# Conditioning columns of a feed-forward layer: where in the layer each of them is reduced

## The chip, the cores and the metric

The kernel runs on one core of a Trainium2 chip. Its time is the device time of one execution in microseconds; several executions of the same program are timed and their median is taken. One further execution is recorded by the hardware profiler, and all rows below come from that one.

## The reference

Three network blocks run one after another on 256 tokens of width 1024: a two-layer block, a block with a recurrence and 32 experts, and a third block. The part that matters here is the feed-forward of the two layers of the first block, and one product of the second block that does not depend on the tokens:

```python
def swiglu(x, w_gate, w_up, w_down):          # 1024 -> 2816 -> 1024, in layer 0 and layer 1
    return (jax.nn.silu(x @ w_gate) * (x @ w_up)) @ w_down

x = layer_norm(ALPHA * x + swiglu(x, w_gate, w_up, w_down), g, b)
...
cond = jax.nn.silu(c)                          # second block: one row of 1024
mod = cond @ ada_w + ada_b                     # 6 * 1024 outputs; the third block has 3 * 1024 more
```

The first 2048 outputs of `mod` are made elsewhere. The other 7168 are 56 columns of 128, each a sum over 1024 products per output.

## The kernel before

**Products in two parts.** Every large weight comes by DMA as float32 and is split into a high part `wh` (ScalarE, L338) and a low part `wl` (L342: every third unit of the feed-forward on GpSimd, the others on VectorE). A unit is 128x1024 numbers of a weight. TensorE then makes three products for each pair (`xh wh`, `xl wh`, `xh wl`), all recorded under L555. The splits are recorded up to three units ahead of the unit that TensorE is at, and four buffers of each of `wh` and `wl` go round.

**The feed-forward, `ffn_ple`.** Its 2816 inner columns are done in six groups `q`: five of 512 columns and a last of 256. In each group the gate product (`dense_F`) is followed by the SiLU on ScalarE (L1153), and the up product by a multiplication on VectorE that reads the up result out of PSUM (`sg<-sg,acc`, L1161) and by a split into `hh` (ScalarE, L593) and `hl` (VectorE, L594). A group of 512 has four units for the gate and four for the up product, the last group two and two. Then `residual` puts ALPHA times the old activations into four PSUM tiles (`acc<-alphaI,xf`, 32 matmuls), and the down product adds 22 units to them (`rows_T`, one unit for each step `k`). PSUM tiles of the name `acc` go round in four buffers: the first three tiles of `residual` take buffers that have long been read, and its last takes the one that the last group's up product was in, so it has to wait for L1161 of that group.

**The conditioning columns.** Each of the 56 columns is one VectorE instruction, L1274: it multiplies a tile `adat` (128x1024, weights) with the row `pe` (the SiLU of c) and sums along the row into one column of `mod2` or `mod3`. TensorE has no part in it. `adat` has three buffers: when column `m` has been recorded, `cond_load` (L1291) puts the load for column `m+3` on SyncE's DMA queue, and that queue also issues the weight loads (L325), in the order in which they were recorded; a load whose buffer isn't free holds up all behind it.

**Where the columns stand.** A table, `MODS`, says for each of the two layers how many columns are pushed at each of its places: entries 0 to 11 behind the gate and the up product of groups 0 to 5 in turn, entry 12 at step 4 of the down product, 13 at step 8, 14 at step 12, 15 at step 16 (entries 16 and 17 are never read). What is pushed at a place is recorded in the background of the next product, one column at each `tick` (one after every unit of gate and up, two in every step of the down product):

```python
            self.cond(MODS[i][2 * q], crow)                      # behind the gate product of group q
            pu = self.dense_F(f"w_ffn_up{i}", x, n=n)
            ...
            self.cond(MODS[i][2 * q + 1], crow)                  # behind the up product and its split
        ps = self.residual(xf)
        ...
        def ready(k):                                            # called at each step of the down product
            if k and k % 4 == 0 and k < NQ - 2:
                self.cond(MODS[i][11 + k // 4], crow)
```

Layer 0 makes 24 of the columns and layer 1 the other 32. The engines run what was recorded for them in that order.

Of the kernel before, what the change touches and what calls it, by code (L numbers as in the profile page):

```python
# [146 lines left out]


EXPERTS = [(1, 0)] + [x for e in range(31) for x in ((1, e + 1), (2, e))] + [(2, 31)]
MODS = [[0, 3] + [2] * 9 + [3] + [0] * 6, [0, 3] + [2] * 9 + [3] + [3, 3, 2, 0, 0, 0]]  # L150


def weight_plan(stages):
# [271 lines left out]
class KB:  # L425
# [709 lines left out]
    def ffn_ple(self, i, xf, x, ready):  # L1135
# [3 lines left out]
        if "mod" in self.stages:  # L1139
            self.push("cond", self.cond_sum(P, i))  # L1140
            crow = self.cond_rows(P, i)
            self.apool = P
            self.ada_end += sum(MODS[i])
        pt = self.tl(P, [128, 2, T], F32, "pt")
# [3 lines left out]
        for q in range(6):  # L1148
# [5 lines left out]
            for _ in range(3 if q == 0 else 0):  # L1154
                self.cond_load()
            self.cond(MODS[i][2 * q], crow)
            pu = self.dense_F(f"w_ffn_up{i}", x, n=n)
            for j in range(n // 256):
# [3 lines left out]
                self.split(gj, hh[:, s], hl[:, s])  # L1162
            self.cond(MODS[i][2 * q + 1], crow)
        ps = self.residual(xf)
# [26 lines left out]
        def ready(k):  # L1191
            if k and k % 4 == 0 and k < NQ - 2:
                self.cond(MODS[i][11 + k // 4], crow)

# [1437 lines left out]
```

## Time and profile before

| | us |
|---|---|
| median of 3 runs | 2259.61 |
| the runs | 2253.85 to 2260.05 |
| the profiled execution | 2253.87 |
| its span, first to last instruction | 2252.1 |
| TensorE busy in the span | 2122.8 (94%) |
| VectorE busy | 1073.3 (48%) |
| ScalarE busy | 724.5 (32%) |
| GpSimd busy | 269.1 (12%) |

Times in the rows are counted from the start of the span. The feed-forward of layer 0 lies between about 227 and 422 us, that of layer 1 between about 564 and 758 us; the experts' weights stream from 1100 to 2000 us. A timeline row gives the start, the busy time, the engine, the line, what was written from what, and in brackets the idle time of the engine just before, with the instruction that ended it.

### The profile page before, as it was taken

What the parts mean: (1) busy time and instruction counts of PE and PEld (TensorE: products, weight loads), DVE (VectorE), ACT (ScalarE), POOL (GpSimd) and SP (SyncE); (2) the same over time, 40 slices, a digit from 0 to 9 for tenths busy, and PEclk for the clock granted to TensorE, in tenths of its full rate; (3) what the DMA queues carried; (4) which work ended last, traced back from release to release, by engine and by line L of the source; (5) the groups of instructions that cost most, each with busy time, mean ns of one, the idle gap of its engine ahead of it and who ended that gap; (6) DMA issues with size and microseconds to landing.
All of it is one profiled execution on the core that took longest, in us unless ns stands there. A gap on an engine that the chain in (4) does not pass through costs nothing. (4 is left out here: it accounts for less than half of the span.)

```text
span 2252.1 us, 31704 instructions
## 1 busy us (share of the span) xinstructions
PE 2122.8 (94%) x13258; PEld 1489.4 (66%) x13258; DVE 1073.3 (48%) x2013; ACT 724.5 (32%) x1169; POOL 269.1 (12%) x144
## 2 busy tenths in 40 slices
PE   8999999999999988799899999999999999999996
PEld 8997997887997878688444444334433333368886
DVE  6775775566787567746222222322221111245665
ACT  5444543554543454343111110111111111133552
POOL 2322232100232012310000000000000000004101
PEclk9999999999999999999899999999999999999999
DMA  7334785332787433105799999999999999984320
GB/s 295 150 146 158 309 315 206 152 150 86 312 319 271 176 122 113 38 1 219 324 426 427 427 423 427 427 428 427 427 428 427 428 427 427 427 333 161 119 76 20
DMA packets 65652, 618.06 MB, mean 274 GB/s; under 512 B 8128, under 2 KB 10176, under 8 KB 19808
## 3 DMA queue, kind: packets, MB, share of 16 engines
q1 hardware_dynamic: 62320, 612.33, 66.5%
q10 hardware_dynamic: 3184, 3.65, 0.5%
q8 instruction: 106, 1.74, 0.3%
q14 instruction: 42, 0.34, 0.0%
HBM read 614.90 MB, written 1.05 MB: 274 GB/s over the span
## 5 line engine op out<-in xcount | busy, mean ns | idle before, releaser
L555 PE MATMUL acc<-xh,wh 128*128 128x256 f32 (+1 forms) x1736 | 487.5, 285 | 7.3 <-ACT wh L338 2.8
L555 PE MATMUL acc<-xl,wh 128*128 128x256 f32 (+1 forms) x1736 | 482.2, 281 | 2.9 <-DVE xl L594 1.5
L555 PE MATMUL acc<-xh,wl 128*128 128x256 f32 (+2 forms) x1704 | 476.4, 280 | 5.3 <-DVE wl L342 5.3
L555 PE MATMUL acc<-expert,xe 128*64 128x512 f32 x2000 | 447.7, 598 | 17.7 <-DMA expert<-exp_w 17.7
L342 DVE TENSOR_TENSOR wl<-w,wh 128x1024 fp32r<-128x1024 f32 x202 | 270.1, 1346 | 155.3 <-ACT wh L338 154.8
L338 ACT ACTIVATE wh<-w 128x1024 fp32r<-128x1024 f32 (+1 forms) x263 | 274.0, 1054 | 213.7 <-PE acc L555 176.0
L555 PEld LDWEIGHTS acc<-xh,wh 128*128 128x128 f32 (+1 forms) x1736 | 326.5, 189 | 16.2 <-issue 5.6
L555 PEld LDWEIGHTS acc<-expert,xe 128*64 128x64 f32 x2000 | 140.5, 137 | 294.8 <-issue 275.5
L555 PEld LDWEIGHTS acc<-xl,wh 128*128 128x128 f32 (+1 forms) x1736 | 328.8, 191 | 7.5 <-DVE xl L594 3.5
L555 PEld LDWEIGHTS acc<-xh,wl 128*128 128x128 f32 (+2 forms) x1704 | 322.5, 189 | 7.1 <-DVE wl L342 6.9
L555 PE MATMUL py<-expert,aT 128*64 128x512 f32 x1024 | 234.3, 600 | 3.6 <-DMA expert<-exp_w 2.8
L342 POOL TENSOR_TENSOR wl<-w,wh 128x1024 fp32r<-128x1024 f32 (+1 forms) x61 | 153.4, 2515 | 527.6 <-ACT wh L338 468.4
L2069 ACT ACTIVATE s<-a 128x512 f32<-128x512 f32 x32 | 20.2, 630 | 530.1 <-DVE a L2068 530.1
L2136 DVE SCALAR_TENSOR_TENSOR xf<-py,mod,xf 128x256 f32<-128x256 f32 x128 | 55.7, 479 | 279.8 <-PE py L555 279.8
L2068 DVE TENSOR_SCALAR a<-acc 128x512 f32<-128x512 f32 x32 | 22.1, 692 | 346.2 <-PE acc L555 346.2
L555 PEld LDWEIGHTS py<-expert,aT 128*64 128x64 f32 x1024 | 72.0, 138 | 137.3 <-issue 127.8
L342 POOL TENSOR_TENSOR wl<-w_w_in,wh 128x1024 fp32r<-128x1024 f32 (+1 forms) x11 | 26.8, 2435 | 1053.8 <-ACT wh L338 1042.9
L1274 DVE SCALAR_TENSOR_TENSOR adat<-adat,pe 128x1024 f32<-128x1024 f32 x56 | 97.3, 1756 | 12.3 <-DMA adat<-tiles 12.3
L2123 ACT ACTIVATE y<-py 64x512 f32<-64x512 f32 x64 | 37.9, 592 | 117.9 <-PE py L555 117.4
L555 PE MATMUL tp<-sel,xh 128*128 128x128 f32 x512 | 63.3, 284 | 7.9 <-ACT aT L2103 6.9
L555 PE MATMUL acc<-wh,hh 128*128 128x512 f32 x176 | 69.7, 396 | 0.0
L555 PE MATMUL acc<-wl,hh 128*128 128x512 f32 x176 | 69.4, 394 | 0.0
(641 smaller groups left out, 2856.2 us busy)
## 6 DMA issues: line engine op xcount, KB each, us to landing
expert<-exp_w SPq DMA_DIRECT2D x188, 2048.0 KB, 31.3
w<-tiles SPq DMA_DIRECT2D x140, 1024.0 KB, 6.9
adat<-tiles SPq DMA_DIRECT2D x56, 512.0 KB, 7.7
w_w_in<-tiles SPq DMA_DIRECT2D x18, 1024.0 KB, 5.0
w<-exp_w SPq DMA_DIRECT2D x3, 2048.0 KB, 7.6
w_w_out<-tiles SPq DMA_DIRECT2D x4, 1024.0 KB, 4.8
expert<-exp_w SPq DMA_DIRECT2D x4, 512.0 KB, 30.1
w_w_o_moba<-tiles SPq DMA_DIRECT2D x2, 1024.0 KB, 4.7
```

The source lines that it names most:

```text
L338: kb.nc.scalar.activation(hi, w, AF.Copy)
L342: (kb.nc.gpsimd if far else kb.nc.vector).tensor_sub(lo, w, hi.bitcast(F32))
L555: self.nc.tensor.matmul(out, lhsT, rhs, start=start, stop=True, skip_group_check=True)
L1274: self.nc.vector.scalar_tensor_tensor(w, w, 1.0, crow[:, int(m >= 48)], op0=OP.mult, op1=OP.mult, accum_out=dst)
L2068: nc.vector.tensor_scalar(a, pg, 7.0, None, op0=OP.min)
L2069: nc.scalar.activation(s, a, AF.Sigmoid, scale=1.702)
L2123: nc.scalar.activation(y[r, o], py[r], AF.Copy)
L2136: nc.vector.scalar_tensor_tensor(xf[:, k], ps[o][:, c], gate2(k), xf[:, k], op0=OP.mult, op1=OP.add)
```

## The change

One table is different; no instruction is added or taken away.

```diff
-MODS = [[0, 3] + [2] * 9 + [3] + [0] * 6, [0, 3] + [2] * 9 + [3] + [3, 3, 2, 0, 0, 0]]
+MODS = [[0, 3, 2, 2, 3, 2, 2, 3, 2, 2, 0, 0] + [3] + [0] * 5, [0, 3, 2, 2, 3, 2, 2, 3, 2, 2, 0, 0] + [3, 3, 3, 2, 0, 0]]
```

In both layers the two columns behind the last gate product (group 5) and the three behind the last up product are gone from there. One more is pushed behind the gate product of group 2 and one more behind the up product of group 3. The other three go to the down product: in layer 0, which had none there, to step 4; in layer 1 the steps 4, 8, 12, 16 have 3, 3, 3, 2 instead of 3, 3, 2, 0.

First VectorE at the end of layer 0's gate and up products, before. `sg` of L1161 is the multiplication of the last group, `adat` of L1274 a column, `wl` of L342 the low part of a weight:

```order
L1274 SCALAR_TENSOR_TENSOR adat_3485,mod_15_119<-adat_3485,pe_2344 128x1024
L342 TENSOR_TENSOR wl_3711<-w_30_3297,wh_3710 128x1024
L1274 SCALAR_TENSOR_TENSOR adat_3580,mod_15_119<-adat_3580,pe_2344 128x1024
L342 TENSOR_TENSOR wl_3745<-w_30_3297,wh_3744 128x1024
L1274 SCALAR_TENSOR_TENSOR adat_3611,mod_15_119<-adat_3611,pe_2344 128x1024
L1274 SCALAR_TENSOR_TENSOR adat_3708,mod_15_119<-adat_3708,pe_2344 128x1024
L1161 TENSOR_TENSOR sg_3741<-sg_3741,acc_3743 128x512
L594 TENSOR_TENSOR hl_2349<-sg_3741,hh_2348 128x512
L342 TENSOR_TENSOR wl_3830<-w_30_3297,wh_3829 128x1024
L1274 SCALAR_TENSOR_TENSOR adat_3739,mod_15_119<-adat_3739,pe_2344 128x1024
L1274 SCALAR_TENSOR_TENSOR adat_3773,mod_15_119<-adat_3773,pe_2344 128x1024
L342 TENSOR_TENSOR wl_3851<-w_31_3426,wh_3850 128x1024
```

The same place now, VectorE:

```order
L342 TENSOR_TENSOR wl_3717<-w_30_3300,wh_3716 128x1024
L1274 SCALAR_TENSOR_TENSOR adat_3586,mod_15_119<-adat_3586,pe_2344 128x1024
L342 TENSOR_TENSOR wl_3751<-w_30_3300,wh_3750 128x1024
L1161 TENSOR_TENSOR sg_3747<-sg_3747,acc_3749 128x512
L594 TENSOR_TENSOR hl_2349<-sg_3747,hh_2348 128x512
L342 TENSOR_TENSOR wl_3830<-w_30_3300,wh_3829 128x1024
L342 TENSOR_TENSOR wl_3849<-w_31_3429,wh_3848 128x1024
L342 TENSOR_TENSOR wl_3881<-w_31_3429,wh_3880 128x1024
L342 TENSOR_TENSOR wl_3897<-w_31_3429,wh_3896 128x1024
L1274 SCALAR_TENSOR_TENSOR adat_3617,mod_15_119<-adat_3617,pe_2344 128x1024
L1274 SCALAR_TENSOR_TENSOR adat_3714,mod_15_119<-adat_3714,pe_2344 128x1024
L1274 SCALAR_TENSOR_TENSOR adat_3745,mod_15_119<-adat_3745,pe_2344 128x1024
```

Two columns no longer stand between the last split of a weight and the multiplication L1161; three stand together some units into the down product.

SyncE's queue over the same stretch, before (`w_33` is a weight tile of the down product):

```order
L325 DMA w_32_3552<-tiles 128x2048 x2
L1291 DMA adat_3580<-tiles 128x1024
L1291 DMA adat_3611<-tiles 128x1024
L325 DMA w_33_3680<-tiles 128x2048 x2
L1291 DMA adat_3708<-tiles 128x1024
L1291 DMA adat_3739<-tiles 128x1024
L1291 DMA adat_3773<-tiles 128x1024
L1291 DMA adat_3804<-tiles 128x1024
L325 DMA w_34_3833<-tiles 128x2048 x2
```

And SyncE's queue now:

```order
L1291 DMA adat_3519<-tiles 128x1024
L325 DMA w_32_3558<-tiles 128x2048 x2
L1291 DMA adat_3586<-tiles 128x1024
L1291 DMA adat_3617<-tiles 128x1024
L325 DMA w_33_3686<-tiles 128x2048 x2
L1291 DMA adat_3714<-tiles 128x1024
L1291 DMA adat_3745<-tiles 128x1024
L325 DMA w_34_3833<-tiles 128x2048 x2
```

Two column loads instead of four stand between `w_33` and `w_34`, and both belong to columns of the down product.

## Rows read from the trace of the kernel before

**Rows 1.** TensorE's waits, 225 to 480 and 560 to 770: total, times, longest

```profile
PE acc L555 <- DVE sg L1161: 5.6, 1, 5.6
...
PE acc L555 <- DVE sg L1161: 5.5, 1, 5.5
```

**Rows 2.** Timeline of TensorE, end of layer 0's up products

```profile
350.27 2.84 PE L555 MATMUL acc<-alphaI,xf 128*128 128x128 f32 x24
358.72 2.07 PE L555 MATMUL acc<-alphaI,xf 128*128 128x128 f32 x8 [5.61 <-DVE sg L1161]
360.44 0.77 PE L555 MATMUL acc<-wh,hh 128*128 128x512 f32 x1
...
364.33 0.40 PE L555 MATMUL acc<-wh,hh 128*128 128x512 f32 x1
```

**Rows 3.** Timeline of TensorE, the same place in layer 1, and its down product's end

```profile
695.82 2.08 PE L555 MATMUL acc<-alphaI,xf 128*128 128x128 f32 x8 [5.49 <-DVE sg L1161]
697.54 0.77 PE L555 MATMUL acc<-wh,hh 128*128 128x512 f32 x1
...
698.86 0.39 PE L555 MATMUL acc<-wh,hh 128*128 128x512 f32 x1
...
758.04 2.32 PE L555 MATMUL py<-pt,w 128*128 128x256 f32 x10
```

**Rows 4.** Stretches of layer 0: length, busy PE, PEld, DVE, ACT, POOL, clock, DMA, GB/s

```profile
357.50:358.00 0.50, 0.00 (x0) 0.00 (x0) 0.50 (x3) 0.00 (x0) 0.00 (x0) 0.50 0.37 148
...
364.20:366.00 1.80, 1.80 (x10) 1.47 (x9) 0.00 (x0) 0.72 (x1) 0.00 (x0) 1.00 1.03 437
```

**Rows 5.** Timeline of VectorE before the last multiplication of layer 0

```profile
348.60 1.21 DVE L342 TENSOR_TENSOR wl<-w,wh 128x1024 fp32r<-128x1024 f32 x1
349.74 3.38 DVE L1274 SCALAR_TENSOR_TENSOR adat<-adat,pe 128x1024 f32<-128x1024 f32 x1
...
356.83 1.23 DVE L1274 SCALAR_TENSOR_TENSOR adat<-adat,pe 128x1024 f32<-128x1024 f32 x1 [3.71 <-DMA adat<-tiles]
...
357.98 0.68 DVE L1161 TENSOR_TENSOR sg<-sg,acc 128x512 f32<-128x512 f32 x1
```

**Rows 6.** Timeline of VectorE, the same place in layer 1

```profile
693.93 1.23 DVE L1274 SCALAR_TENSOR_TENSOR adat<-adat,pe 128x1024 f32<-128x1024 f32 x1 [3.57 <-DMA adat<-tiles]
```

**Rows 7.** SyncE's queue, timeline; then DMA issues of 347 to 349, time to landing last

```profile
346.48 0.80 SPq L325 DMA_DIRECT2D w<-tiles  x2
347.37 11.05 SPq L1291 DMA_DIRECT2D adat<-tiles  x4
...
adat<-tiles SPq DMA_DIRECT2D x2, 512.0 KB, 9.3
```

**Rows 8.** All 56 columns: shortest, median and longest in ns

```profile
L1274 DVE SCALAR_TENSOR_TENSOR adat<-adat,pe x56: 1207/1220/3430, 257.2 to 734.5; 128x1024 f32<-128x1024 f32 x56
```

**Rows 9.** Timeline of VectorE in layer 0, groups 2 and 4: weight splits it waited for

```profile
294.39 1.22 DVE L342 TENSOR_TENSOR wl<-w,wh 128x1024 fp32r<-128x1024 f32 x1 [2.25 <-ACT wh L338]
...
330.29 1.23 DVE L342 TENSOR_TENSOR wl<-w,wh 128x1024 fp32r<-128x1024 f32 x1 [0.92 <-ACT wh L338]
...
337.86 1.22 DVE L342 TENSOR_TENSOR wl<-w,wh 128x1024 fp32r<-128x1024 f32 x1 [0.71 <-ACT wh L338]
```

**Rows 10.** Timeline of GpSimd: the last up unit's split in layer 0, and the next

```profile
343.42 3.03 POOL L342 TENSOR_TENSOR wl<-w,wh 128x1024 fp32r<-128x1024 f32 x1 [8.51 <-ACT wh L338]
348.88 3.15 POOL L342 TENSOR_TENSOR wl<-w,wh 128x1024 fp32r<-128x1024 f32 x1 [2.44 <-ACT wh L338]
```

**Rows 11.** Timeline of VectorE in layer 1's down product

```profile
721.60 3.23 DVE L1274 SCALAR_TENSOR_TENSOR adat<-adat,pe 128x1024 f32<-128x1024 f32 x1 [1.85 <-DMA adat<-tiles]
...
725.90 1.22 DVE L342 TENSOR_TENSOR wl<-w,wh 128x1024 fp32r<-128x1024 f32 x1
```

**Rows 12.** Experts' stretch, columns as in rows 4; SyncE's waits, 800 to 1110

```profile
1100.00:2000.00 900.00, 869.87 (x4197) 354.98 (x4197) 192.74 (x424) 111.61 (x209) 0.00 (x0) 0.99 1.00 423
...
SPq L412 <- PE acc L555: 31.7, 5, 19.5
```

## The prediction

> **What bounds the kernel now.** I read TensorE's waits first, since it is busy for 94% of the span. In the two stretches that hold a feed-forward, one wait stands out in each: 5.6 us and 5.5 us, both for L1161, the multiplication of an up result on VectorE [rows 1]. The other waits of those stretches are 0.5 us or less. So TensorE sets the pace there, and no weight split ever held it up.
>
> TensorE's timeline shows which multiplication it is. The first 24 of `residual`'s 32 matmuls run from 350.27 to 353.11 us; the last eight start at 358.72 [rows 2]. They need the PSUM tile of group 5's up product, which L1161 of that group frees. VectorE's timeline shows why it is late: the up product ends at 350.27, but VectorE starts a column at 349.74 that takes 3.38 us, then has another in front whose weights arrive only at 356.83, after 3.71 us of idling, and only then, at 357.98, comes L1161 [rows 5]. SyncE's queue explains the late weights: that load was issued at 347.37, behind the weight load of 346.48, and took 9.3 us to land [rows 7]. Layer 1 repeats the pattern, with 3.57 us for the load [rows 6] and 5.49 us on TensorE [rows 3].
>
> The wait costs more than itself. While TensorE sat idle its granted clock fell to half (0.50 at 357.5, which is 1.2 GHz); it is back at 1.00, 2.4 GHz, from 364.2 [rows 4], and the matmuls in between are slow.
>
> **What the change takes away.** First the waits: 5.61 + 5.49 = 11.10 us [rows 2, 3]. Then the slow matmuls.
> - At full clock, 24 of `residual`'s matmuls take 2.84 us [rows 2], so eight take 0.95; after the wait they took 360.44 - 358.72 = 1.72. Lost: 0.77 in each layer.
> - The down product at full clock: 22 units of 12 matmuls are 264, and from the fourth on 261 take 758.04 - 698.86 = 59.18 us [rows 3], 0.227 each. In layer 0 the first nine took 364.33 - 360.44 = 3.89 instead of 2.04 [rows 2]. Lost: 1.85. In layer 1 the first three took 1.32 instead of 0.68 [rows 3]. Lost: 0.64.
>
> That is 2 x 0.77 + 1.85 + 0.64 = 4.03 us, and 11.10 + 4.03 = **15.1 us** in all.
>
> **Is the wait really gone?** In the new order VectorE has, between the last multiplications of group 4 and L1161 of group 5, column, split, column, split. These are the four that now end at 349.81 [rows 5]. The up product ends at 350.27, so L1161 can start some 0.2 us later and, at 0.68 us [rows 5], is done by about 351.2. TensorE needs the tile at 353.11. The 24 matmuls that need nothing cover it with 1.9 us to spare, so I take 0 for what is left of the wait. If VectorE came to that place later than now, only what exceeds 1.9 us would be paid. Neither of the two columns still there waits for a late load: the one that did belonged to the load behind `w_33`, and in the new queue only columns of the down product are behind `w_33`.
>
> **What it costs where the columns go.** A column takes between 1.21 and 3.43 us, 1.22 in the median [rows 8]. The long ones lie beside a GpSimd split: one that begins at 349.74, with GpSimd at a split from 348.88 to 352.03, took 3.38 [rows 5, 10]. The Trainium skill (GPSIMD Engine Reference, section Specifications) says that GpSimd shares its SBUF interfaces with VectorE and that VectorE instructions with two SBUF inputs contend with it; a column has two such inputs, `adat` and `pe`. By that rule every column that meets a GpSimd split would be a long one, which speaks against putting more of them between splits. By it and the rows the five moved columns of a layer would take up to 5 x 3.43 = 17.2 us of VectorE instead of 5 x 1.22 = 6.1. The trace agrees for the long ones, but shows most columns in gaps. What follows uses both durations from the rows.
>
> - *Third column behind gate 2.* It runs during up 2. VectorE waits 2.25 us there for the next weight split [rows 9]. At 1.22 us the column fits; at 3.43 it pushes the split by 1.2 us, and splits run units ahead. I take 0.
> - *Third column behind up 3.* It runs during gate 4. VectorE's idle time from there to the end of group 4 is 0.92 + 0.71 = 1.63 us [rows 9], so 1.22 fits with little over. Behind it is the tightest place I found: group 4's multiplications release ScalarE, which then feeds GpSimd the split of the last up unit, done at 343.42 + 3.03 = 346.45 [rows 10]. That unit starts 24 matmuls before 350.27; a unit takes 12 x 0.227 = 2.72 us, so at 347.55, and first reads the low part 0.2 us later. Slack: about 1.3 us. At 1.22 the cost is 0; at 3.43 VectorE is 1.8 us late and TensorE waits 0.5 us per layer; if the column also had to wait 3.7 us for its weights, as the worst did [rows 5], it would be 5.5 - 1.3 = 4.2 us per layer. I take 0, since the two loads in question are issued well ahead in the new queue (three columns ahead, none directly behind a blocked weight load), and keep 4.2 as the end of the range.
> - *Down product.* Layer 1 already has groups of three there, with a column that waited 1.85 us for its load and then took 3.23 [rows 11], and TensorE never waited [rows 1]. How near was it? The split that followed (unit 12 of 0 to 21, counted back over VectorE's and GpSimd's splits from the last) was done at 725.90 + 1.22 = 727.12 [rows 11]; unit 12 starts ten units before 758.04 [rows 3], at 730.8. Slack 3.6 us. Layer 0's one group and layer 1's 3, 3, 3, 2 are of the same kind, and the columns that used to run at the start of the down product (the three pushed behind up 5) are gone. Cost 0; the other bound is under the rivals.
> - *Loads.* As many as before, of the same size. Column loads are earlier by one or two places in groups 2 to 4, and `w_34` no longer waits for a column of the down product's start. I take 0.
>
> **Does it reach the end?** The experts run at a DMA share of 1.00 for 900 us [rows 12], so time won before could be lost if that stream began at a fixed moment. It doesn't: before it, the expert loads wait for TensorE (31.7 us in five waits, for buffers it has to free) [rows 12], so they begin earlier by as much as TensorE does.
>
> **Sum.** The profiled execution took 2253.87 us, which is 1.77 around its span. 2253.87 - 15.1 = 2238.8. It lay 5.7 us under the median of the three runs, 2259.61; from the median, 2259.61 - 15.1 = 2244.5. I forecast **2244 us**.
>
> **Rivals.**
> - *A smaller wait replaces it.* The moved column of up 3 meets a GpSimd split and a late load, VectorE reaches group 4's multiplications late, and TensorE waits at the last up unit: 4.2 us per layer, 15.1 - 8.4 = 6.7 gained, 2252.9. For it: only 1.6 us of idle time covers the column. Against: the loads of this place are ahead by three columns. At 3.43 us without the load it would be 1.0 in all, 2245.5.
> - *Only the wait goes, the slow clock stays.* Some other break near the place, too short to count as one of the waits above, leaves the clock at half for as long as now. Gain 11.1, 2248.5. For it: the clock is the part I can't trace to one instruction. Against: the stretches before 353 and after 364 run at full clock with the same short breaks.
> - *Nothing arrives.* The gain is lost before the end, because the order of expert loads or of the third block's weights is set by something other than TensorE: 2259.6. Against: rows 12.
> - *Slower.* VectorE falls behind wherever the columns went, because each moved column is held to 3.43 us and each group waits 3.71 us for its first load. Up 3's column then costs 8.4 us in both layers. A group of three in the down product takes 3 x 3.43 + 3.71 = 14.0 us; four units of TensorE last 10.9, of which VectorE's own 8/3 splits of 1.22 take 3.3, which leaves 7.6, and the slack covers 3.6 more; 2.8 us remain for TensorE. Five such groups (counting the pair as one) are 14.0. 8.4 + 14.0 - 15.1 = 7.3 us slower, 2266.9. It outweighs the gain once columns cost about two thirds of that beyond the cover. Against: layer 1 ran such groups without a wait. The sharing that the Trainium skill states (GPSIMD Engine Reference, section Specifications) would make the longer duration the usual one wherever a GpSimd split runs.
> - *The change doesn't do what it says*, that is, something else stands in front of L1161 and is just as late. The new order shows splits alone between the last column and L1161, so I give it no chance of its own.
>
> **How the numbers follow.** Chances: forecast 0.74, smaller wait 0.10, clock 0.06, nothing 0.05, slower 0.05. The range takes in the forecast on either base (2238.8 and 2244.5) with some 3 us below, since single runs of one program here differ by up to 6 us, and reaches up to the smaller wait: 2236 to 2253. About 0.3%, 6.8 us, is what a measurement of this kernel can tell from no change. The forecast, the clock rival and the better half of the smaller wait are faster by more than that, with a little off for what I overlooked: 0.85. Within it: 0.10. Slower: 0.05.
>
> **What would show it.** In the changed profile TensorE's waits in the feed-forwards have no entry for L1161 of more than 1 us; `residual`'s 32 matmuls run as one block of some 3.8 us; the granted clock stays at 1.00 through the start of both down products; L1161 of group 5 starts right after the up product, with no column before it that waited for DMA. Wrong it would be if TensorE waits for `wl` in the last up unit, or in the down product behind a group of columns, or if the experts' stream starts at the same time as before.

## The result and the profile after

The median went from 2259.61 to **2244.0 us** (five runs, 2241.32 to 2247.12), a ratio of 0.9937 with a 95% interval of 0.9921 to 0.9953: 0.6% faster. The profiled execution took 2241.32 us.

First the waits, since the prediction hung on one of them. TensorE's waits from 225 to 480 us, then from 560 to 770 (total, times, longest):

```profile
PE py L555 <- ACT pr L1123: 1.4, 1, 1.4
PE tp L756 <- DVE xf L743: 0.5, 1, 0.5
PE acc L555 <- ACT xh L593: 0.2, 1, 0.2
...
PE acc L555 <- DVE xl L594: 0.3, 1, 0.3
```

L1161, with 5.6 and 5.5 us before [rows 1], is gone from both layers. None of what is left waits for a weight split; the 1.4 us for `pr` are not new, before has them at 486.20, outside these stretches. Then TensorE's timeline at the end of the up products of layer 0 and of layer 1, in place of [rows 2, 3]:

```profile
352.13 0.28 PE L555 MATMUL acc<-xh,wl 128*128 128x256 f32 x1
352.25 3.73 PE L555 MATMUL acc<-alphaI,xf 128*128 128x128 f32 x32
355.73 0.48 PE L555 MATMUL acc<-wh,hh 128*128 128x512 f32 x1
...
680.94 3.73 PE L555 MATMUL acc<-alphaI,xf 128*128 128x128 f32 x32
684.43 0.48 PE L555 MATMUL acc<-wh,hh 128*128 128x512 f32 x1
```

All 32 rows of `residual` are one block now, and the first matmuls of the down product start 3.48 us after it began, where before they started 10.17 us after. VectorE's timeline shows why, in place of [rows 5]: column, split, and then L1161, which waits for TensorE and no longer the other way round.

```profile
349.43 1.21 DVE L1274 SCALAR_TENSOR_TENSOR adat<-adat,pe 128x1024 f32<-128x1024 f32 x1
...
350.58 1.22 DVE L342 TENSOR_TENSOR wl<-w,wh 128x1024 fp32r<-128x1024 f32 x1
352.44 0.69 DVE L1161 TENSOR_TENSOR sg<-sg,acc 128x512 f32<-128x512 f32 x1 [0.65 <-PE acc L555]
```

To compare kernels I use one **stretch** in each layer: from the first `acc<-alphaI,xf` (the up products are done) to the first `py<-pt,w` (the down product is done). Stretches of the kernel before, with the columns of [rows 4] (length, busy PE, PEld, DVE, ACT, POOL, granted clock, DMA share, GB/s):

```profile
350.27:422.15 71.88, 66.27 (x298) 55.32 (x297) 29.84 (x38) 22.80 (x22) 16.14 (x7) 0.95 0.50 192
687.49:758.04 70.55, 65.06 (x299) 54.46 (x297) 42.94 (x54) 22.82 (x22) 16.92 (x8) 0.98 0.66 248
```

And of the kernel after:

```profile
352.25:415.67 63.42, 63.42 (x298) 53.14 (x297) 28.00 (x34) 22.80 (x22) 16.71 (x7) 1.00 0.50 202
415.67:680.94 265.27, 257.10 (x1994) 237.85 (x1992) 197.91 (x349) 145.44 (x259) 38.57 (x16) 0.99 0.55 211
680.94:744.36 63.42, 63.42 (x298) 53.14 (x297) 39.07 (x50) 22.82 (x22) 18.64 (x8) 1.00 0.67 260
```

Both layers now take the same 63.42 us, with TensorE busy for all of it at 1.00, which is 2.4 GHz: 8.46 us less in layer 0, 7.13 less in layer 1, 15.6 in all. The medians differ by 15.6 too, but that they agree to a tenth is luck: the interval of the ratio leaves 10.6 to 17.9 us. Between the two stretches nothing moved (265.27 us, and 687.49 - 422.15 = 265.34 before). The spans, 2252.1 and 2239.5, differ by only 12.6, because in code that the change doesn't touch this one execution lost 1.98 us ahead of 352.25 and 1.08 behind 744.36. Part of the first is this, at the start of layer 0's gate products, a stretch which had 1.00 before:

```profile
228.26:240.00 11.74, 11.66 (x85) 11.40 (x85) 8.28 (x14) 7.04 (x11) 0.00 (x0) 0.85 1.00 398
```

### The profile page after: what moved, and what is told of

Same layout as the page of the kernel before. It is cut to its first block, busy times and chain, and to the rows that moved or that the text cites. A ratio compares the mean times of both kernels' runs of the same rounds, so it can differ in the third digit from the quotient of the medians.

```text
span 2239.5 us, 31711 instructions
## 1 busy us (share of the span) xinstructions
PE 2120.7 (95%) x13258; PEld 1489.4 (67%) x13258; DVE 1077.1 (48%) x2013; ACT 724.3 (32%) x1169; POOL 273.5 (12%) x144
## 5 line engine op out<-in xcount | busy, mean ns | idle before, releaser
L342 DVE TENSOR_TENSOR wl<-w,wh 128x1024 fp32r<-128x1024 f32 x202 | 267.6, 1334 | 145.2 <-ACT wh L338 144.7
L342 POOL TENSOR_TENSOR wl<-w,wh 128x1024 fp32r<-128x1024 f32 (+1 forms) x61 | 157.0, 2573 | 510.9 <-ACT wh L338 467.7
L342 POOL TENSOR_TENSOR wl<-w_w_in,wh 128x1024 fp32r<-128x1024 f32 (+1 forms) x11 | 26.7, 2430 | 1054.2 <-ACT wh L338 1043.3
L1274 DVE SCALAR_TENSOR_TENSOR adat<-adat,pe 128x1024 f32<-128x1024 f32 x56 | 102.7, 1853 | 6.6 <-DMA adat<-tiles 6.5
```

Of the source, the lines that this page charges most:

```text
L342: (kb.nc.gpsimd if far else kb.nc.vector).tensor_sub(lo, w, hi.bitcast(F32))
L1274: self.nc.vector.scalar_tensor_tensor(w, w, 1.0, crow[:, int(m >= 48)], op0=OP.mult, op1=OP.mult, accum_out=dst)
```

## The experiments

The table has each kernel's two stretches, TensorE's wait for L1161 in layer 0 and in layer 1, and the time. Ratios are to runs of the kernel before on the same chip and in the same batch, whose medians were 2258.62 us (for e1 to e4), 2259.06 (e5, e6, e7, e9), 2259.1 (e8, e10) and 2261.1 (e11); two kernels were run once only.

| kernel | stretches, us | wait, us | time, us | ratio (95%) |
|---|---|---|---|---|
| before | 71.88, 70.55 | 5.61, 5.49 | 2259.61 | |
| after | 63.42, 63.42 | none | 2244.0 | 0.9937 (0.9921 to 0.9953) |
| e1_pair_only | 63.42, 63.43 | none | 2242.25 | 0.9933 (0.9914 to 0.9952) |
| e2_three_only | 70.97, 70.53 | 5.43, 5.32 | 2257.8 | 0.9994 (0.9979 to 1.001) |
| e3_layer0 | 63.42, 70.89 | none, 5.48 | 2251.26 | 0.9957 (0.9936 to 0.9977) |
| e4_layer1 | 71.30, 63.43 | 5.83, none | 2249.35 | 0.996 (0.9943 to 0.9977) |
| e5_no_load_wait | 65.54, 65.54 | 1.81, 1.81 | 2245.23 | 0.9936 (0.9916 to 0.9956) |
| e6_no_gpsimd_there | 71.69, 71.58 | 5.61, 5.30 | 2259.07 | one run |
| e7_busy_wait | 74.15, 74.15 | none | 2265.52 | 1.0026 (1.0012 to 1.0039) |
| e11_busy_24 | 68.80, 68.79 | none | 2256.5 | 0.9984 (0.9968 to 1.0) |
| e9_one_back | 64.38, 64.38 | 0.69, 0.69 | 2245.54 | one run |
| e8_crowded | 63.43, 63.45 | none | 2251.77 | 0.9965 (0.9953 to 0.9978) |
| e10_no_gpsimd_split | 63.43, 63.43 | none | 2244.39 | 0.9939 (0.9922 to 0.9956) |

### Which part of the change carries the gain

**e1_pair_only** moves only the pair behind the last gate, and leaves the three behind the last up where they were.

```diff
-MODS = [[0, 3] + [2] * 9 + [3] + [0] * 6, [0, 3] + [2] * 9 + [3] + [3, 3, 2, 0, 0, 0]]
+MODS = [[0, 3, 2, 2, 3, 2, 2, 3, 2, 2, 0, 3] + [0] * 6, [0, 3, 2, 2, 3, 2, 2, 3, 2, 2, 0, 3] + [3, 3, 2, 0, 0, 0]]
```

> One part alone: in both layers only the two columns behind gate 5 go (one behind gate 2, one behind up 3); the three behind up 5 stay and the down product keeps its old table. Theory: the wait came from the two columns that stood before the last multiplication, so this part carries the whole gain: the stretch from the end of the up products to the end of the down product is 63.4 us in each layer (71.9 and 70.6 before), and the time is that of the changed kernel, 2244 within noise, 15 us under before. Rival: the three columns that no longer sit between the start of the down product and its loads carry a part of it (they put four column loads on SyncE's queue in front of a weight load): then a stretch stays 1 us or more longer than 63.4.

**e2_three_only** does the other part alone.

```diff
+MODS = [[0, 3] + [2] * 9 + [0] + [3] + [0] * 5, [0, 3] + [2] * 9 + [0] + [3, 3, 3, 2, 0, 0]]
```

> The other part alone: in both layers only the three columns behind up 5 go to the down product; the two behind gate 5 stay. Theory: nothing changes before the last multiplication, so the wait stays at 5.5 us and the clock falls as before: stretches of 71.9 and 70.6, 2259.6 within noise. Rival, the loads: with fewer column loads on the queue the late one lands earlier, and the wait shrinks by more than 1 us.

**e3_layer0** and **e4_layer1** make the whole change in one layer each.

```diff
# e3_layer0
+MODS = [[0, 3, 2, 2, 3, 2, 2, 3, 2, 2, 0, 0] + [3] + [0] * 5, [0, 3] + [2] * 9 + [3] + [3, 3, 2, 0, 0, 0]]
# e4_layer1
+MODS = [[0, 3] + [2] * 9 + [3] + [0] * 6, [0, 3, 2, 2, 3, 2, 2, 3, 2, 2, 0, 0] + [3, 3, 3, 2, 0, 0]]
```

> The change in layer 0 alone. Theory: the layers are independent; stretches of 63.4 in layer 0 and 70.6 in layer 1; 8.5 us under before by the traces (8.2 by the sum of the prediction), about 2251. Rival: what layer 0 wins is given back before the end; then under 4 us.

> The change in layer 1 alone. Theory: stretches of 71.9 in layer 0 and 63.4 in layer 1; 7.1 us under before by the traces (6.9 by the sum), about 2252.5. Rival: only the two changes together pay; then under 3 us.

The pair alone gives stretches of 63.42 and 63.43 us and the whole gain. The three alone leave the wait, and what they do to the time can't be measured. TensorE's timeline in layer 0 of e2_three_only is that of [rows 2] over again:

```profile
351.04 2.84 PE L555 MATMUL acc<-alphaI,xf 128*128 128x128 f32 x24
359.31 2.07 PE L555 MATMUL acc<-alphaI,xf 128*128 128x128 f32 x8 [5.43 <-DVE sg L1161]
361.03 0.77 PE L555 MATMUL acc<-wh,hh 128*128 128x512 f32 x1
```

The layers add up: by the stretches 8.46 in the one and 7.12 in the other, by the times 7.4 and 9.3 us, each known to within 4 to 5 us. Moving the three columns to the down product is neither a part of the gain nor a price.

### The load or the column's own time

**e5_no_load_wait** keeps all columns at their old places, but the one that stands right in front of L1161 has no load: it reads a blank tile.

```diff
+            if q == 2:
+                self.blank = self.tl(self.xpool, [128, 2, 1024], F32, "xn")[:, 0]
+                nc.gpsimd.memset(self.blank, 0.0)
...
+            if r in (20, 44):
+                self.adat[16 + r] = self.blank
+                return
```

> The kernel before, without the load of one column in each layer, the second of the two that stand before the last multiplication; that column is computed on a tile of zeros (GpSimd writes it in group 2), so one conditioning column of each layer is wrong and 0.5 MB less is read per layer. It keeps both columns' own time and takes away only the wait for the load (3.7 us). Theory: the columns alone make L1161 late by 1.9 us beyond the cover: the two columns end at about 354.2 in place of 358.0, TensorE waits 1.9 us in each layer, the clock doesn't fall, the stretches are 65.3 us, the time is 11.7 under before, about 2248. Rival: the columns' own time is what counts and the load was late only on paper; then the wait stays above 4 us.

VectorE's timeline in e5_no_load_wait: the same two columns as in [rows 5], one of 3.38 and one of 1.21 us, without the 3.71 us between them.

```profile
351.42 3.38 DVE L1277 SCALAR_TENSOR_TENSOR adat<-adat,pe 128x1024 f32<-128x1024 f32 x1
...
354.73 1.21 DVE L1277 SCALAR_TENSOR_TENSOR xn<-xn,pe 128x1024 f32<-128x1024 f32 x1
...
355.88 0.68 DVE L1164 TENSOR_TENSOR sg<-sg,acc 128x512 f32<-128x512 f32 x1
```

TensorE's timeline there, and the stretch that holds the wait:

```profile
351.96 2.84 PE L555 MATMUL acc<-alphaI,xf 128*128 128x128 f32 x24
356.61 1.16 PE L555 MATMUL acc<-alphaI,xf 128*128 128x128 f32 x8 [1.81 <-DVE sg L1164]
357.52 0.48 PE L555 MATMUL acc<-wh,hh 128*128 128x512 f32 x1
...
351.96:360.00 8.04, 6.23 (x45) 5.60 (x44) 7.08 (x8) 1.58 (x2) 1.76 (x1) 1.00 0.90 341
```

The wait falls to 1.81 us and the clock stays at 1.00 right behind it. So without the late load 3.8 of the 5.6 us are gone and so is the fall of the clock; the 1.8 us that are left come from the two columns' own time. While the load is late, the length of the first column doesn't count, as the next run shows.

**e6_no_gpsimd_there** asks whether the long column is to blame: it takes from GpSimd the one split beside which the 3.38 us column runs, and gives it to VectorE.

```diff
-... or name[:5] == "w_ffn" and r0 + c0)
+... or name[:5] == "w_ffn" and r0 + c0 and not (name[:10] == "w_ffn_down" and r0 + 128 * k0 == 256))
```

> The kernel before, with the one weight split that GpSimd does beside the last two columns (unit 2 of each down product) done by VectorE. Theory: the first of the two columns then takes 1.22 us instead of 3.38, but the second still waits for its load until 356.8, so L1161 and the wait of 5.5 us stay; no gain. Rival: GpSimd's hold on VectorE is a part of the wait; then the wait is 2 us shorter in each layer, 3.5.

VectorE's timeline in e6_no_gpsimd_there:

```profile
349.38 1.21 DVE L1274 SCALAR_TENSOR_TENSOR adat<-adat,pe 128x1024 f32<-128x1024 f32 x1
...
350.52 1.21 DVE L342 TENSOR_TENSOR wl<-w,wh 128x1024 fp32r<-128x1024 f32 x1
356.47 1.23 DVE L1274 SCALAR_TENSOR_TENSOR adat<-adat,pe 128x1024 f32<-128x1024 f32 x1 [4.74 <-DMA adat<-tiles]
```

The column is short, and nothing is won: the load arrives when it arrives, and VectorE idles 4.74 us for it where it idled 3.71. The rival that put the wait down to GpSimd falls.

### What the slow clock costs

**e7_busy_wait** and **e11_busy_24** leave the columns as before and put work into TensorE's wait: matmuls of identity by identity, 48 and 24 of them, whose result nobody reads.

```diff
+                if h and t and warm:
+                    p = self.tl(self.pp, [128, 128], F32, "tp")
+                    for _ in range(warm):
+                        self.mm(p, self.ident, self.ident, start=True)
...
-        ps = self.residual(xf)
+        ps = self.residual(xf, warm=48)
```

> The kernel before, with 48 matmuls of the identity into a spare PSUM tile put before the last eight of residual, so that TensorE has work of about 5.6 us during the wait. The wait for L1161 itself stays. Theory: the clock stays at full rate, and only the slow matmuls' loss comes back: stretches of 69.3 (layer 0, 2.6 less) and 69.1 (layer 1, 1.4 less), 4 us under before. Rival: the clock falls at this place whatever TensorE does; then 71.9 and 70.6, no gain.

I had taken a row for a matmul: the 48 float32 matmuls left 96 rows, and filled 10.7 us instead of the 5.6 I wanted. The kernel got slower by the longer filling, so its time says nothing of the clock's cost. Half as many fit:

> The kernel before with half the filling of the run before: 24 float32 matmuls of identity by identity, 48 passes in the trace, stand in `residual` of each feed-forward right before the last tile's, so in the place of the wait for L1161. At the 0.11 us of a pass in that run they take about 5.3 us, a little less than the waits they replace (5.61 and 5.49). The theory, that an idle TensorE is what lowers the granted clock: at most 0.4 us of wait is left, the clock stays at 1.00, and the stretch from the end of the up products to the end of the down product is 63.4 + 5.6 = 69.0 us in layer 0 and 63.4 + 5.5 = 68.9 in layer 1, against 71.88 and 70.55 before: some 4.5 us off the time, 0.2%, about what can be measured. The rival, that the clock falls there for some other reason than the idling (the change of the kind of matmul, or the start of the down product): the clock falls all the same, the stretches are 71.9 and 70.6, and the time is that of the kernel before.

TensorE's timeline in layer 0 of e11_busy_24, and the stretch from there:

```profile
355.09 2.84 PE L555 MATMUL acc<-alphaI,xf 128*128 128x128 f32 x24
357.77 5.52 PE L555 MATMUL tp<-ident 128*128 128x128 f32 x48
363.13 1.06 PE L555 MATMUL acc<-alphaI,xf 128*128 128x128 f32 x8
...
363.13:380.00 16.87, 16.87 (x81) 14.13 (x80) 9.00 (x11) 6.77 (x7) 3.35 (x2) 1.00 0.51 179
```

The late load is still there (the second column waited 3.73 us for it), and TensorE begins the last eight rows 8.04 us after the up products ended, where before it was 8.45. But it was busy meanwhile, and the clock stays at 1.00. The stretch, 68.80, is that of after plus the filling: 63.42 + (363.13 - 357.77) = 68.78. In e7_busy_wait it is 63.42 + 10.72 = 74.14, measured 74.15. So working through the gap instead of idling through it saved 71.88 - 68.80 = 3.08 us in layer 0 and 1.76 in layer 1. The filling is 0.25 and 0.13 shorter than the waits were, so **2.83 and 1.63 us** are what the slow clock and the restart cost. The times can't carry this: e11_busy_24 is 4.6 us under its own runs of before, with an interval that reaches no change at all; it rests on the stretches. That the clock falls here because TensorE idled, and not at a place of the program, is shown by these two kernels; that 1.81 us of idling at this place doesn't lower it, by e5_no_load_wait.

### How near the change is to the edge

**e9_one_back** is the kernel after with one column put back behind the last gate.

```diff
+MODS = [[0, 3, 2, 2, 3, 2, 2, 3, 2, 2, 1, 0] + [2] + [0] * 5, [0, 3, 2, 2, 3, 2, 2, 3, 2, 2, 1, 0] + [3, 3, 3, 1, 0, 0]]
```

> The changed kernel with one column put back behind gate 5 in each layer (taken from the down product's last group). Its load isn't behind the late weight load. Theory: it stands right before L1161 and beside a GpSimd split, so it takes 3.4 us; L1161 ends at about 355.8 on the clock of the changed trace, where TensorE needs the tile at 355.1: a wait of 0.7 us in each layer, stretches of 64.1, no fall of the clock. Rival: one column fits into the cover of 1.9 us; no wait.

VectorE's timeline in layer 0 of e9_one_back, then TensorE's:

```profile
350.68 3.40 DVE L1274 SCALAR_TENSOR_TENSOR adat<-adat,pe 128x1024 f32<-128x1024 f32 x1
...
354.01 0.68 DVE L1161 TENSOR_TENSOR sg<-sg,acc 128x512 f32<-128x512 f32 x1
...
354.74 1.16 PE L555 MATMUL acc<-alphaI,xf 128*128 128x128 f32 x8 [0.69 <-DVE sg L1161]
```

A single column there, even a long one with its load in time, costs TensorE 0.69 us of wait, and the stretch 0.96. The time that the prediction called spare is real, if a little shorter than 1.9 us: L1161 began 2.80 us after the up products ended (354.01 - 351.21) instead of 0.19, so 2.61 us later, and the stretch lost only 0.96 of them. Some 1.65 us were covered.

**e8_crowded** pushes three columns at each place from the first up to the fifth gate, 24 in a layer where the change has 21, with none behind the fifth up. (The expectation says up 4 for the last of the eight places; in the table it is gate 4.)

```diff
+MODS = [[0, 3, 3, 3, 3, 3, 3, 3, 3, 0, 0, 0] + [0] * 6, [0, 3, 3, 3, 3, 3, 3, 3, 3, 0, 0, 0] + [3, 3, 2, 0, 0, 0]]
```

> All columns of the gate and up products put behind up 0 to up 4, three at each of eight places (six in a group instead of five or four), none in layer 0's down product. The price of the slower rival measured by itself. In the changed kernel VectorE still idles about 3 us in a group, most of it short waits for ScalarE; a further column is 1.2 to 3.4 us, and three buffers with loads of up to 9 us allow about six columns in a group of 21.8 us. Theory: VectorE comes to the end of its reserve, TensorE waits 0 to 3 us in each layer before the last group; the stretch from there to the end of the down product stays 63.4; 0 to 6 us over the changed kernel. Slower rival: every column is long and waits for its load; 5 us or more in each layer.

By the medians it is 7.8 us above after, by the ratios 6.3, so 3 to 4 in each layer: at the upper end of the theory or just beyond, and under the rival. TensorE's waits in layer 0 of e8_crowded, one of them in its timeline, and the stretch around it:

```profile
PE acc L555 <- DVE wl L342: 2.7, 3, 1.5
...
319.23 0.39 PE L555 MATMUL acc<-xh,wl 128*128 128x256 f32 x1 [1.47 <-DVE wl L342]
...
310.00:320.00 10.00, 8.53 (x73) 8.23 (x72) 9.92 (x9) 4.83 (x6) 4.65 (x2) 1.00 0.90 333
```

These are weight splits that VectorE makes too late: from 310 to 320 us it is busy for 9.92 of 10. So the rival's mechanism exists, and three columns a layer more than the change has are enough to meet it. In this execution, the slowest of the ten, the gate and up products took 128.54 and 129.00 us, against 123.11 in layer 1 of after: 5.4 and 5.9 more, of which 2.7 and 3.1 are waits. A part of the rest lies in slower matmuls without a wait, told of in the last section.

**e10_no_gpsimd_split** is the kernel after with all weight splits of the feed-forwards on VectorE.

```diff
-... or name == "w_in_3" and c0 != 928 or name[:5] == "w_ffn" and r0 + c0)
+... or name == "w_in_3" and c0 != 928)
```

> The changed kernel with all weight splits of the two feed-forwards on VectorE instead of every third on GpSimd. Theory: the long columns (up to 3.4 us) are those that meet a GpSimd split; without it all 56 take 1.2 us. VectorE's work in a group of 21.8 us is then 8 splits of 1.22, 4.1 us of multiplications and splits of activations, 4 or 5 columns of 1.22: 20 us, so it still keeps up: 2244 within noise. Rival: long columns have another cause (DMA writing into SBUF); then columns over 2 us remain, and with more work on VectorE the time grows by several us.

All 56 columns of e10_no_gpsimd_split, in place of [rows 8]:

```profile
L1274 DVE SCALAR_TENSOR_TENSOR adat<-adat,pe x56: 1215/1219/1227, 257.7 to 730.8; 128x1024 f32<-128x1024 f32 x56
```

And of after:

```profile
L1274 DVE SCALAR_TENSOR_TENSOR adat<-adat,pe x56: 1210/1220/3452, 259.2 to 731.6; 128x1024 f32<-128x1024 f32 x56
```

Without GpSimd's splits no column takes longer than 1.23 us, so it is they that stretch columns to 3.45. The time, 2244.39 us, is that of after: VectorE's own extra splits and the shorter columns are both under cover. The Trainium skill (GPSIMD Engine Reference, section Specifications) states that the two engines share SBUF interfaces. This run agrees: 3.45 us at the longest beside GpSimd's splits, 1.23 without them.

## Why the prediction was right

**The bound and the wait.** TensorE was taken to set the pace, with one wait in each layer to remove. Both waits are gone, and nothing stands in their place. L1161 was to be done 1.9 us before TensorE needs its tile. It ended at 352.44 + 0.69 = 353.13, and the last eight rows of `residual` begin 24 times 0.109 us behind 352.25, at 354.86: 1.7 us. e9_one_back uses them up.

**The slow clock, mis-sized by a little.** The term was 4.03 us. The stretches shrank by 8.46 and 7.13; less the waits, 5.61 and 5.49, that leaves 2.85 and 1.64, together 4.49. e11_busy_24, set against the same two waits, gives 2.83 and 1.63: filled time costs its own length and nothing more. What the step left out, 0.23 in each layer, is a tail: 24 rows that last 2.84 us [rows 2] begin 3.48 / 32 = 0.109 us apart, 2.61 in all, so the last one ends 0.23 after the next would have begun. When TensorE stops, this overlap is lost too. Two smaller slips of the step all but cancel: eight rows take 0.87 us at full clock and not 0.95, and the down product's first three matmuls take 0.78 and not 0.68 (356.51 - 355.73). With the tail the sum of 15.1 becomes 15.6 for the execution that it was read from. In others the loss behind the wait is another: 2.12 and 1.79 us in e2_three_only, 2.66 and 2.86 in e6_no_gpsimd_there (stretch less 63.42 less the wait). So in each layer the loss can be about 1 us away from what one execution shows, and that the sum agrees better than that is luck.

**A slip without effect.** The prediction, like the description of the kernel before, speaks of 32 matmuls in `residual`. They are 16 float32 matmuls, and the trace shows each as two rows. The durations were taken from rows, so the sum doesn't change; e7_busy_wait, sized by matmuls, missed for that reason.

**What the moved columns cost.** Taken as 0, and 0 was measured. Behind gate 2 the added column is a long one, 3.06 us; group 2's first multiplication comes 0.89 us later against the end of the up products than before, and splits run far enough ahead. Behind up 3 the prediction had little room for the third column and feared a long one. There the added column, at 330.13, took 1.22 us; the long ones beside it were there before (3.42 us each, at 324.81 and 332.58). VectorE's timeline of after, layer 0:

```profile
294.27 3.06 DVE L1274 SCALAR_TENSOR_TENSOR adat<-adat,pe 128x1024 f32<-128x1024 f32 x1 [0.27 <-DMA adat<-tiles]
...
326.78 3.42 DVE L1274 SCALAR_TENSOR_TENSOR adat<-adat,pe 128x1024 f32<-128x1024 f32 x1
...
330.13 1.22 DVE L1274 SCALAR_TENSOR_TENSOR adat<-adat,pe 128x1024 f32<-128x1024 f32 x1
...
335.26 2.90 DVE L1274 SCALAR_TENSOR_TENSOR adat<-adat,pe 128x1024 f32<-128x1024 f32 x1 [0.43 <-DMA adat<-tiles]
...
340.97 0.68 DVE L1161 TENSOR_TENSOR sg<-sg,acc 128x512 f32<-128x512 f32 x1
```

VectorE's idle time up to group 4's multiplications shrank from 1.63 us [rows 9] to 0.95 (0.43 + 0.52), and the last long column from 3.42 to 2.90: together 1.20 us, what the added column took. So group 4's first multiplication begins 11.28 us before the up products end (352.25 - 340.97), as before (350.27 - 339.00 = 11.27), and GpSimd's split of the last up unit begins 6.87 us before that end (345.38), against 6.85 before [rows 10]. In the down product of layer 0 the third column of the group took 3.41 us; in layer 1 one waited 1.88 us for its load and took 3.19, much as before [rows 11]. TensorE has no wait for a split in either. The bounds of 4.2 us a layer and of 2.8 a group were not reached.

**The rivals.** A smaller wait: no wait for `wl` in the feed-forwards. The clock staying slow: 1.00 through both stretches; it fell with the wait, as e11_busy_24 shows. Nothing arrives: the 265 us between the stretches are unchanged, so layer 1 kept what layer 0 had won; the experts' loads, whose start the prediction named as a sign, begin at 1030.16 us instead of 1042.96, 12.8 earlier, and of the rest the times say that it arrived. Slower: its mechanism needs more columns than the change puts there (e8_crowded).

**Argued and not shown.** Why the load was late, behind a blocked weight load in SyncE's queue, was read from [rows 7]; e5_no_load_wait shows what the lateness costs, and no kernel took the queue apart. The traces lead one step further back, to GpSimd. The longest wait of SyncE's queue in before, 330 to 350 us:

```profile
SPq L325 <- POOL wl L342: 7.3, 1, 7.3
```

The weight load of 346.48 went out when GpSimd's split of the last up unit ended, at 346.45 [rows 10]. After has the same pair (348.42 and 348.45) and lost nothing by it, since only columns of the down product stand behind that load. In e10_no_gpsimd_split it goes out 5.70 us before the up products end (350.56 - 344.86) instead of 3.80 (352.25 - 348.45). Whether a GpSimd split less would have been a cure of its own in the old order was not tried.

## What to carry to other kernels

Work that runs in the background is free only where nothing stands in line behind it that the bounding engine waits for: before the last product of a stage, look at what the vector queue holds between its last split and the operation that frees the accumulator. A background operation whose load may be late is worse there than a long one, since an idle TensorE can pay again in a lower clock; here 11.1 us of waits cost 15.6. The cure may be a single number, but its neighbours have an edge too: one column back cost 1 us a layer, three more in the middle 3 to 4 by the times.

## What the hardware did that was not expected

**Idling and the clock.** At this place waits of 0.69 (e9_one_back) and 1.81 us (e5_no_load_wait) left the granted clock at 1.00, waits of 5.3 to 5.8 us lowered it each time: wherever there was one, in before, e2, e3, e4 and e6, the first matmul of the down product took 0.77 us instead of 0.48. How long the slow part then lasts varies for equal waits: the stretch of layer 0 lost 8.46 us in before and 7.55 in e2_three_only, with waits of 5.61 and 5.43. Elsewhere in the program the length of a single wait doesn't decide. In before a wait of 2.71 us that ended at 116.17 left the clock at 1.00, while one of 1.58 us that ended at 497.00 was followed by 0.55:

```profile
116.17:119.00 2.83, 2.83 (x27) 2.66 (x28) 2.79 (x7) 0.00 (x0) 0.84 (x1) 1.00 0.90 371
...
497.00:500.00 3.00, 3.00 (x14) 2.67 (x15) 2.04 (x8) 1.77 (x8) 0.00 (x0) 0.55 0.02 5
```

The fall at the start of layer 0's gate products in after, told of with the result, came behind three waits of 0.23, 0.53 and 0.25 us. What decides in these places was not tried.

**A pace 4% slower at full granted clock.** In two of the thirteen profiled executions the matmuls of the gate and up products follow each other every 0.1177 us instead of 0.1133 for ten microseconds and more. Two stretches of 10 us in e8_crowded, TensorE busy throughout, with 87 and 91 matmuls:

```profile
320.00:330.00 10.00, 10.00 (x87) 10.00 (x86) 9.14 (x11) 1.82 (x3) 2.96 (x1) 1.00 0.95 360
340.00:350.00 10.00, 10.00 (x91) 10.00 (x90) 9.72 (x11) 3.15 (x3) 2.86 (x1) 1.00 0.88 344
```

In layer 0 it lasted from about 291 to 301 us and from 316 to 337, which is some 1.1 of the 5.4 us by which that layer was longer; the waits, 2.7 us of idling and the slower matmuls of each restart, make the rest. Layer 1 has it too, from 627 to 633 us and from 670 to the end of the up products. In e11_busy_24 all of layer 0's gate and up products from 245 to 345 us ran so; in before and after nothing from 245 to 345 or from 580 to 680 did. The granted clock reads 1.00 in these stretches of either kind. What sets it stays open; no experiment was made on it.
